# Quarter-array values, shared low-rank visits and shifted pieces in a streamed encoder layer on one Trainium2 core

## The chip, the cores and the metric

The kernel runs on one core of a Trainium2 chip. The metric is device time in microseconds (us); the number for a kernel is the median of its timed runs. One more execution is taken by the hardware profiler, and all times inside the kernel come from that one.

## What is computed

One encoder layer of width 2048 for 256 tokens. RMS-normed input `h` goes through one wide projection; three token mixers work on slices of it (windowed attention, a bidirectional RWKV-7 scan, cross-attention to 256 memory tokens); each result is gated, projected, weighted by a merge gate and summed; an output projection and a residual add close the layer. All in float32. The loop over both directions is the RWKV branch; the two products in it are the low-rank ones, and for each direction a scan over the tokens follows it, with a 64x64 state per head.

```python
h = rms_norm(x, norm_g)
proj = h @ w_in
...
mkv = rms_norm(mem, mem_norm_g) @ x_w_kv
...
for d in range(N_DIR):
    wd = -softplus(-(w0[d] + tanh(w_in[d]) @ w2[d])) - 0.5
    ad = sigmoid(a0[d] + a_in[d] @ a2[d])
    kd = k * (1.0 + (ad - 1.0) * k_a)
...
merged = gates[0] * (y_a @ attn_w_o) + gates[1] * (y_r @ rwkv_w_o) + gates[2] * (y_x @ x_w_o)
return x + merged @ w_out
```

## The kernel before

Nearly all of the work is products of 256 tokens with 160 MB of weights. The weights are cut into 277 **pieces**, each 128 partitions by 1024 numbers (512 KB); the first two are half as large (`planned(w_kv[0], KT, 512, 2)`: two single pieces of one k-tile). A piece passes through four stations:

- SyncE (SP) issues its DMA into one of four `raw` buffers (L172);
- ScalarE (ACT) rounds it to `w_hi` (L187), VectorE (DVE) computes the rest, `w_lo` (L191); four buffers of each;
- TensorE (PE) multiplies. In `stream_tok` tokens lie on the partitions of the result: per piece eight matmuls of 512 columns with `w_hi` (L287 and L288, with the high and low part of the activations) and four with `w_lo` (L280). The low products of a piece are issued one piece later (`late`), those of a stream's last piece at its end. `stream_feat` (L261, L262, L254) is the same with features on the partitions and 256 columns. Each stream has two accumulators, `ps[0]` and `ps[1]`, which `evac` takes away at its end.

After each piece `advance()` (L224) gives every background generator its turn: attention and, later, three RWKV batches b = 0, 1, 2 of four heads, one after the other. A generator that yields n sleeps for n pieces. What its steps put on PE stands between two pieces; I call it a **visit**. The order of PE and SP is the order of the code; on DVE and ACT too, after the attention part. There it matters that a step of a generator and the casts of the stream stand in one queue.

The steps of an RWKV batch that the change or the prediction names:

- norms of kk (L765), the low-rank products of the two head pairs (`low_rank(0)`, `low_rank(1)`, L777, evacuated by ACT tanh, L781), and the transposes of the norm (L795), with which DVE multiplies kk (L796);
- `prepare(d)` for each direction, in three blocks a piece apart. Block A: DVE sum and scan (L809, L812). Block B: ACT exponentials and kd (L817 to L821), then DVE kd (L823). Block C: DVE aa (L825) and four operations into BK (L829 to L832). `prepare(0)` of batch b+1 runs while batch b is in its state chain;
- `values()` (L854): 16 small products with the identity, which turn v to token order; ACT copies them into SV (L857, L858);
- products L877 and L880; the inversion of 64x64 blocks, first on DVE (L943, L946), then with X going out to memory (`td`) and back (L959), a transpose on DVE (L965, TP) and small products L971 and L978;
- the state chain over four chunks c of 64 tokens: Z (L1013, copied by DVE at L1015), U (L1023, copied into SV by DVE at L1025 and ACT at L1026), S (L1031, to Sn on DVE at L1035 and L1037, copied into SV by ACT at L1038 and DVE at L1039), each step a visit with a `yield 1` behind it. Each step needs the copy of the step before;
- outputs (L1004, L1007), norm and gate.

`ps_b` is the PSUM pool of these steps and has four buffers. `beside` (L161) holds the loads of memory and token rows (`araw`), each tied to the number of a piece: they are issued ahead of that piece. `WARM` matmuls on zeros (L328) stand ahead of everything on PE.

Of the kernel before, what the change touches and what calls it, by code (L numbers as in the profile page):

```python
# [8 lines left out]
F32 = mybir.dt.float32  # L9
# [8 lines left out]
P = 128  # L18
T = 256
DM = 2048  # L20
KT = DM // P
C = 64
NCH = T // C
# [26 lines left out]
RAWS = 4  # L50
HB = 4
LB = 4
WARM = 16

INV_STEP = 3

# [2 lines left out]
def tile_hybrid_layer(ctx: ExitStack, tc: tile.TileContext, x_tok, xT, memT, w_kv, wt, wq2, wf, wg, gate_b,  # L59
                      wo_a, wo_r, wo_x, w_out, lora, par, rowp, consts, out):  # L60
    nc = tc.nc
    V, S, G, TE = nc.vector, nc.scalar, nc.gpsimd, nc.tensor
# [25 lines left out]
    ident = cst[:, 0:128]  # L88
# [25 lines left out]
    def planned(w, kt, c, small=0, ks=None):  # L114

        n, ks = 1024 // c, ks or list(range(kt))
        for j in list(range(0, small)) + list(range(small, len(ks), n)):
            m = 1 if j < small else n
            plan.append((w[:, ks[j] : ks[j] + m, :], ks[j : j + m], c))
# [9 lines left out]
        planned(wo_x[c], 4, 512)  # L129


    planned(w_kv[0], KT, 512, 2)
    planned(w_kv[1], KT, 512)
    planned(wt[0], KT, 512)
    planned(wt[1], KT, 512)
# [135 lines left out]
    def stream_tok(kt, c, act, evac, ks=None):  # L271

        ah, al = act
        ps = [ps_acc.tile([P, 512], F32, name="acc") for _ in range(2)]
        ks = ks or list(range(kt))

        def low(lo, kl):
            for i in range(2):
                for k, kk in enumerate(kl):
                    TE.matmul(ps[i][:, 0:c], ah[:, kk, i * P : (i + 1) * P], lo[:, k, :], start=False, stop=(kk == ks[-1]))  # L280

        late = None
        for kl, hi, lo in pieces(c, ks):
            for i in range(2):
                for k, kk in enumerate(kl):
                    m = slice(i * P, (i + 1) * P)
                    TE.matmul(ps[i][:, 0:c], ah[:, kk, m], hi[:, k, :], start=(kk == ks[0]), stop=False)  # L287
                    TE.matmul(ps[i][:, 0:c], al[:, kk, m], hi[:, k, :], start=False, stop=False)  # L288
            if late is not None:
                low(*late)  # L290
            late = lo, kl
            advance()
        low(*late)
        for i in range(2):
            evac(i, ps[i][:, 0:c])


# [66 lines left out]
    ss4 = [apool.tile([P, 4, T], F32, name="ss4", bufs=1) for _ in range(2)]  # L364
    part_m = prep(memT, "mem_g", mT_, ss4[0], True)
    part_x = prep(xT, "norm_g", hT, ss4[1], False)
    for piece, k0, n in ((0, 0, 1), (1, 1, 1), (2, 2, 2), (3, 4, 4), (5, 8, 4), (7, 12, 4)):
        beside[piece] = [lambda k0=k0, n=n: part_m(k0, n)]
    for piece, k0 in ((11, 0), (13, 4), (16, 8), (18, 12)):
        beside[piece] = [lambda k0=k0: part_x(k0, 4)]  # L370

    kmT = apool.tile([P, 4, T], F32, name="kmT")
# [371 lines left out]
    def rwkv_batch(b):  # L744
# [4 lines left out]
        rp, kp, vp = (rkv[n, b] for n in "rkv")  # L749
# [22 lines left out]
        def low_rank(p):  # L772
            lps = [ps_b.tile([P, 512], F32, name="ps_b") for _ in range(2)]
            for j, s in enumerate((th, afT)):
                for d in range(2):
                    dr = slice(64 * d, 64 * d + 64)
                    TE.matmul(lps[d][:, j * T : (j + 1) * T], lw[dr, p, j, :], s[dr, :], start=True, stop=True)  # L777
            for d in range(2):
                f = rev if d else (lambda a: a)
                o = d * 6 + pps[p]  # L780
                S.activation(f(sgs[d][:, p, :]), lps[d][:, 0:T], AF.Tanh, bias=der[:, 52 + o : 53 + o], scale=0.5)  # L781
                S.activation(f(aas[d][:, p, :]), lps[d][:, T : 2 * T], AF.Tanh, bias=der[:, 64 + o : 65 + o], scale=0.5)

        yield 1
        low_rank(0)
        yield 2
        low_rank(1)
        rb = tpool.tile([P, 8, 64], F32, name="t1")
        S.copy(rb, rn.unsqueeze(2).broadcast_to([P, 8, 64]))
        yield 2  # L790
        rps = ps_b.tile([P, 2, T], F32, name="ps_b")
        for p in range(2):
            for t in range(2):
                o = 4 * p + 2 * t
                TE.transpose(rps[:, p, t * P : (t + 1) * P], rb[:, o : o + 2, :].rearrange("p a b -> p (a b)"), ident)  # L795
        V.tensor_tensor(kk, kk, rps, ALU.mult)  # L796
        yield 1

        def chs(ap):
# [46 lines left out]

        def values():

            vps = ps_b.tile([P, 2, NCH, 64], F32, name="ps_b")
            for p in range(2):  # L850
                for c in range(NCH):
                    for e in range(2):
                        er, orr = slice(64 * e, 64 * e + 64), slice(64 - 64 * e, 128 - 64 * e)
                        TE.matmul(vps[orr, p, c, :], vp[er, p, c * C : (c + 1) * C], ident[er, er], start=True, stop=True)  # L854
            for e in range(2):
                orr = slice(64 - 64 * e, 128 - 64 * e)
                S.copy(SV[e][orr, :, 0], vps[orr])  # L857
                S.copy(SV[e][orr, :, 1, ::-1], vps[orr])  # L858

        def arrive(d):  # L860
            f, E, BK = prep[d]
# [100 lines left out]
        yield 2  # L962

        TP = rpool.tile([P, 16, 32], F32, name="TP")
        V.transpose(TP.rearrange("p u s -> p (u s)"), Xu[:, :, 0:32])  # L965
        yield 1
        lo_, up = [slice(e * 64, e * 64 + 32) for e in range(2)], [slice(e * 64 + 32, e * 64 + 64) for e in range(2)]
# [41 lines left out]
        for c in range(NCH):  # L1009
# [6 lines left out]
            if c == NCH - 1:  # L1016
                yps += [ps_b.tile([P, 2, 2, 64], F32, name="ps_b") for _ in range(2)]
                outputs((1, 2))
            yield 1

            ups = [ps_b.tile([P, 2, 64], F32, name="ps_b") for _ in range(2)]
            for q, e in turns:
# [150 lines left out]
    for c in (3, 0, 1, 2):  # L1173
# [18 lines left out]
        def evac(i, ps, c=c, grt=grt, act=act):  # L1192
            gated(grt[:, i, :], ps)
            V.tensor_tensor(act[:, i, :], act[:, i, :], grt[:, i, :], ALU.add)
            start(merge(c, i, act))
# [100 lines left out]
```

## Time and profile before

| | us |
|---|---|
| timed runs (3) | 910.26, 910.92, 912.34 |
| median | 910.92 |
| profiled execution | 907.79 |
| its span | 906.0 |
| PE busy in the span | 893.4 |
| DVE busy | 648.2 |
| ACT busy | 456.9 |

In a row of the timeline stand the start, the busy time, engine, line, operation, output and inputs with their shapes, the number of instructions, and in brackets the idle time ahead of it with what ended that. The matmuls of PE overlap, so a matmul's time is read from one start to the next. L numbers are lines of the kernel before.

### The profile page before, as it was taken

What the parts mean: (1) busy time and instruction counts of PE and PEld (TensorE: products, weight loads), DVE (VectorE), ACT (ScalarE), POOL (GpSimd) and SP (SyncE); (2) the same over time, 40 slices, a digit from 0 to 9 for tenths busy, and PEclk for the clock granted to TensorE, in tenths of its full rate; (3) what the DMA queues carried; (4) which work ended last, traced back from release to release, by engine and by line L of the source; (5) the groups of instructions that cost most, each with busy time, mean ns of one, the idle gap of its engine ahead of it and who ended that gap; (6) DMA issues with size and microseconds to landing.
All of it is one profiled execution on the core that took longest, in us unless ns stands there. A gap on an engine that the chain in (4) does not pass through costs nothing.

```text
span 906.0 us, 15781 instructions
## 1 busy us (share of the span) xinstructions
PE 893.4 (99%) x6204; PEld 757.8 (84%) x6204; DVE 648.2 (72%) x1074; ACT 456.9 (50%) x690; POOL 89.5 (10%) x104
## 2 busy tenths in 40 slices
PE   8999999999999999999999999999999999999998
PEld 6788978999789999877899987788887778888886
DVE  6867687765488898666797955789796658586442
ACT  7766566655565544543554345355433435444331
POOL 2254231210100011100001110010000000000000
PEclk9999999999999999999999999999999999999999
DMA  8857644434656556644456575456768545787771
GB/s 303 268 195 252 199 140 137 141 120 136 185 179 206 165 177 191 183 128 145 146 180 216 162 235 147 129 165 185 223 198 244 163 152 176 238 272 233 233 234 66
DMA packets 67977, 168.66 MB, mean 186 GB/s; under 512 B 24448, under 2 KB 25984, under 8 KB 67904
## 3 DMA queue, kind: packets, MB, share of 16 engines
q1 hardware_dynamic: 42336, 150.75, 53.0%
q10 hardware_dynamic: 25568, 16.91, 6.5%
q8 instruction: 49, 0.80, 0.4%
q14 instruction: 24, 0.20, 0.1%
HBM read 160.82 MB, written 6.82 MB: 185 GB/s over the span
## 4 chain that ended last, share of the span: by engine, by line
PE 92%; DVE 3%; DMA 2%; issue 1%; ACT 1%; SPq 0%; ACTq 0%; DVEq 0%
PE acc L287 20%; PE acc L280 19%; PE acc L288 19%; PE acc L261 8%; PE acc L254 8%; PE acc L262 8%; PE ps_b L877 1%; DVE w_lo L191 1%; PE ps_t L448 1%; PE ps_b L880 1%; PE ps_b L1004 1%; DMA araw<-in_memT 1%; PE ps_s L544 1%; PE ps_b L777 1%; PE ps_b L1013 1%
## 5 line engine op out<-in xcount | busy, mean ns | idle before, releaser
L191 DVE TENSOR_TENSOR w_lo<-raw,w_hi 128x1024 fp32r<-128x1024 f32 (+1 forms) x277 | 342.2, 1248 | 94.9 <-PE acc L280 40.9
L187 ACT CAST w_hi<-raw 128x1024 fp32r<-128x1024 f32 (+1 forms) x277 | 286.5, 1046 | 200.3 <-PE acc L288 70.0
L287 PE MATMUL acc<-w_hi,hT 128*128 128x512 f32 (+1 forms) x512 | 200.1, 393 | 0.0
L288 PE MATMUL acc<-w_hi,hT 128*128 128x512 f32 (+1 forms) x512 | 195.3, 384 | 0.0
L261 PE MATMUL acc<-hT,w_hi 128*128 128x256 f32 x576 | 141.9, 285 | 0.2 <-DVE gx L1092 0.2
L262 PE MATMUL acc<-hT,w_hi 128*128 128x256 f32 x576 | 140.6, 283 | 0.0
L280 PE MATMUL acc<-w_lo,hT 128*128 128x512 f32 (+1 forms) x512 | 133.2, 385 | 0.0
L287 PEld LDWEIGHTS acc<-w_hi,hT 128*128 128x128 f32 x512 | 96.3, 188 | 21.0 <-issue 1.3
L261 PEld LDWEIGHTS acc<-hT,w_hi 128*128 128x128 f32 x576 | 110.3, 192 | 1.8 <-issue 1.7
L288 PEld LDWEIGHTS acc<-w_hi,hT 128*128 128x128 f32 x512 | 96.4, 188 | 17.5
L262 PEld LDWEIGHTS acc<-hT,w_hi 128*128 128x128 f32 x576 | 110.4, 192 | 0.1
L280 PEld LDWEIGHTS acc<-w_lo,hT 128*128 128x128 f32 x512 | 93.6, 188 | 19.0 <-issue 0.3
L254 PE MATMUL acc<-hT,w_lo 128*128 128x256 f32 x576 | 80.1, 285 | 0.0
L287 PE MATMUL acc<-w_hi,mT 128*128 128x512 f32 x192 | 76.7, 400 | 2.5 <-ACT w_hi L187 2.4
L288 PE MATMUL acc<-w_hi,mT 128*128 128x512 f32 x192 | 75.7, 394 | 0.0
L254 PEld LDWEIGHTS acc<-hT,w_lo 128*128 128x128 f32 x576 | 73.7, 192 | 0.9 <-issue 0.7
L280 PE MATMUL acc<-w_lo,mT 128*128 128x512 f32 x192 | 51.8, 395 | 0.0
L287 PEld LDWEIGHTS acc<-w_hi,mT 128*128 128x128 f32 x192 | 36.1, 188 | 13.0 <-ACT w_hi L187 4.3
L280 PEld LDWEIGHTS acc<-w_lo,mT 128*128 128x128 f32 x192 | 36.1, 188 | 8.7
L288 PEld LDWEIGHTS acc<-w_hi,mT 128*128 128x128 f32 x192 | 36.1, 188 | 8.2
L287 PE MATMUL acc<-w_hi,ya 128*128 128x512 f32 x96 | 38.1, 397 | 0.0
L288 PE MATMUL acc<-w_hi,ya 128*128 128x512 f32 x96 | 37.5, 390 | 0.0
(241 smaller groups left out, 981.1 us busy)
## 6 DMA issues: line engine op xcount, KB each, us to landing
raw<-in_wg SPq DMA_DIRECT2D x96, 512.0 KB, 3.8
raw<-in_wf SPq DMA_DIRECT2D x72, 512.0 KB, 4.0
raw<-in_w_out SPq DMA_DIRECT2D x32, 512.0 KB, 4.3
raw<-in_wt SPq DMA_DIRECT2D x24, 512.0 KB, 4.5
raw<-in_w_kv SPq DMA_DIRECT2D x15, 512.0 KB, 5.2
raw<-in_wo_a SPq DMA_DIRECT2D x12, 512.0 KB, 5.6
raw<-in_wo_r SPq DMA_DIRECT2D x12, 512.0 KB, 4.6
raw<-in_wo_x SPq DMA_DIRECT2D x8, 512.0 KB, 3.7
```

Source lines behind the costliest of these rows:

```text
L187: S.copy(hi_t[m], raw_t[m])
L191: V.tensor_tensor(lo_t[m], raw_t[m], hi_t[m].bitcast(F32), ALU.subtract)
L254: TE.matmul(ps[i][:, 0:T], lo[:, k, i * P : (i + 1) * P], ah[:, kk, :], start=False, stop=(kk == kt - 1))
L261: TE.matmul(ps[i][:, 0:T], hi[:, k, m], ah[:, kk, :], start=(kk == 0), stop=False)
L262: TE.matmul(ps[i][:, 0:T], hi[:, k, m], al[:, kk, :], start=False, stop=False)
L280: TE.matmul(ps[i][:, 0:c], ah[:, kk, i * P : (i + 1) * P], lo[:, k, :], start=False, stop=(kk == ks[-1]))
L287: TE.matmul(ps[i][:, 0:c], ah[:, kk, m], hi[:, k, :], start=(kk == ks[0]), stop=False)
L288: TE.matmul(ps[i][:, 0:c], al[:, kk, m], hi[:, k, :], start=False, stop=False)
L448: TE.transpose(ps[:, kt * T + t * P : kt * T + (t + 1) * P], pr[:, t, kt * P : (kt + 1) * P], ident)
L544: TE.matmul(s_ps[:, t, :], qT[r, pair, t * P : (t + 1) * P], kTt[r, g, :], start=True, stop=True)
L777: TE.matmul(lps[d][:, j * T : (j + 1) * T], lw[dr, p, j, :], s[dr, :], start=True, stop=True)
L877: TE.matmul(apss[e][:, c, :], BK[er, p, c, :], AR[er, p, d, c, :], start=True, stop=True)
```

## The change

Seven edits:

1. `WARM` goes from 16 to 22.
2. The first weight starts with four single pieces instead of two (278 pieces in all), and the keys of `beside` move up by one, so that each load stands ahead of the same weights.
3. `stream_tok`: at a stream's last piece the low products of the piece before are held back. The visit comes first, then for each accumulator the low products of both last pieces, then its evacuation.
4. `low_rank(0)` joins the visit of the norms, the transposes (L795) follow two pieces later, and `low_rank(1)` joins their visit. From the norms to block A three pieces pass (1, 1, 1) where six did (1, 2, 2, 1).
5. `values()` writes two PSUM tiles instead of one, in the order c, p, e, and the quarter of the array changes with each product: four in a row use four different quarters, where before two alternated. ACT copies eight halves instead of four wholes.
6. For b = 2 one more piece passes before the DVE transpose TP.
7. Behind Z of chunk 0 the generator sleeps two pieces instead of one, for b = 0 and 1.

```diff
-WARM = 16
+WARM = 22
...
-    planned(w_kv[0], KT, 512, 2)
+    planned(w_kv[0], KT, 512, 4)
...
-        def low(lo, kl):
-            for i in range(2):
-                for k, kk in enumerate(kl):
-                    TE.matmul(ps[i][:, 0:c], ah[:, kk, i * P : (i + 1) * P], lo[:, k, :], start=False, stop=(kk == ks[-1]))
-
-        late = None
+        def low(i, lo, kl):
+            for k, kk in enumerate(kl):
+                TE.matmul(ps[i][:, 0:c], ah[:, kk, i * P : (i + 1) * P], lo[:, k, :], start=False, stop=(kk == ks[-1]))
+
+        late = []
...
-            if late is not None:
-                low(*late)
-            late = lo, kl
+            if late and kl[-1] != ks[-1]:
+                l = late.pop(0)
+                for i in range(2):
+                    low(i, *l)
+            late.append((lo, kl))
             advance()
-        low(*late)
+
         for i in range(2):
+            for l in late:
+                low(i, *l)
             evac(i, ps[i][:, 0:c])
...
-    for piece, k0, n in ((0, 0, 1), (1, 1, 1), (2, 2, 2), (3, 4, 4), (5, 8, 4), (7, 12, 4)):
+    for piece, k0, n in ((0, 0, 1), (1, 1, 1), (2, 2, 2), (4, 4, 4), (6, 8, 4), (8, 12, 4)):
...
-        yield 1
         low_rank(0)
-        yield 2
-        low_rank(1)
+        yield 1
         rb = tpool.tile([P, 8, 64], F32, name="t1")
         S.copy(rb, rn.unsqueeze(2).broadcast_to([P, 8, 64]))
-        yield 2
+        yield 1
...
         V.tensor_tensor(kk, kk, rps, ALU.mult)
+        low_rank(1)
         yield 1
...
-            vps = ps_b.tile([P, 2, NCH, 64], F32, name="ps_b")
-            for p in range(2):
-                for c in range(NCH):
+            vps = [ps_b.tile([P, NCH, 64], F32, name="ps_b") for _ in range(2)]
+            for c in range(NCH):
+                for p in range(2):
                     for e in range(2):
-                        er, orr = slice(64 * e, 64 * e + 64), slice(64 - 64 * e, 128 - 64 * e)
-                        TE.matmul(vps[orr, p, c, :], vp[er, p, c * C : (c + 1) * C], ident[er, er], start=True, stop=True)
+                        er, o = slice(64 * e, 64 * e + 64), 64 * (1 - e ^ p)
+                        TE.matmul(vps[p][o : o + 64, c, :], vp[er, p, c * C : (c + 1) * C], ident[er, er], start=True, stop=True)
...
+        if b == 2:
+            yield 1
         V.transpose(TP.rearrange("p u s -> p (u s)"), Xu[:, :, 0:32])
...
-            yield 1
+            yield 2 if c == 0 and b < 2 else 1
```

What stands in the queues at three places. First VectorE at the hand-over from batch 0 to batch 1, chunk 1 to 2 of batch 0, before:

```order
L823 TENSOR_TENSOR kd<-kd,rs_k 128x512
L191 TENSOR_TENSOR w_lo<-raw,w_hi 128x1024
L1035 TENSOR_TENSOR Sn<-ps_b,Sn 128x256
L1037 TENSOR_TENSOR Sn<-Sn,EC 128x256
L1039 COPY SV_2825<-Sn 64x4x64
L825 SCALAR_TENSOR_TENSOR aa<-aa,kk 128x512
L829 SCALAR_TENSOR_TENSOR BK<-aa,Ei 64x8x64
L830 SCALAR_TENSOR_TENSOR BK<-aa,Ei 64x8x64
L831 TENSOR_TENSOR BK<-kd,Ei 64x8x64
L832 TENSOR_TENSOR BK<-kd,Ei 64x8x64
L191 TENSOR_TENSOR w_lo<-raw,w_hi 128x1024
L1015 COPY Z<-ps_b 128x256
```

and in the changed kernel, whose lines are numbered up to seven higher (SV copies L1032, Sn L1042 and L1044, Z L1022):

```order
L1032 TENSOR_SCALAR SV_2780<-ps_b 64x2x64 x2
L827 SCALAR_TENSOR_TENSOR aa<-aa,kk 128x512
L831 SCALAR_TENSOR_TENSOR BK<-aa,Ei 64x8x64
L832 SCALAR_TENSOR_TENSOR BK<-aa,Ei 64x8x64
L833 TENSOR_TENSOR BK<-kd,Ei 64x8x64
L834 TENSOR_TENSOR BK<-kd,Ei 64x8x64
L191 TENSOR_TENSOR w_lo<-raw,w_hi 128x1024
L1042 TENSOR_TENSOR Sn<-ps_b,Sn 128x256
L1044 TENSOR_TENSOR Sn<-Sn,EC 128x256
L1046 COPY SV_2781<-Sn 64x4x64
L191 TENSOR_TENSOR w_lo<-raw,w_hi 128x1024
L1022 COPY Z<-ps_b 128x256
```

Block C of batch 1 stood between the Sn of chunk 1 and the Z copy of chunk 2; it now stands between the SV copies and the Sn of chunk 1.

Second, VectorE at the hand-over from batch 1 to batch 2, before:

```order
L1039 COPY SV_4860<-Sn 64x4x64
L825 SCALAR_TENSOR_TENSOR aa<-aa,kk 128x512
L829 SCALAR_TENSOR_TENSOR BK<-aa,Ei 64x8x64
L830 SCALAR_TENSOR_TENSOR BK<-aa,Ei 64x8x64
L831 TENSOR_TENSOR BK<-kd,Ei 64x8x64
L832 TENSOR_TENSOR BK<-kd,Ei 64x8x64
L191 TENSOR_TENSOR w_lo<-raw,w_hi 128x1024
L1015 COPY Z<-ps_b 128x256
```

and now, from the last operations on the state of chunk 0 to the SV copies of chunk 1:

```order
L825 TENSOR_TENSOR kd<-kd,rs_k 128x512
L108 SCALAR_TENSOR_TENSOR ga<-ga,acc 128x512 x2
L191 TENSOR_TENSOR w_lo<-raw,w_hi 128x1024
L1022 COPY Z<-ps_b 128x256
L827 SCALAR_TENSOR_TENSOR aa<-aa,kk 128x512
L831 SCALAR_TENSOR_TENSOR BK<-aa,Ei 64x8x64
L832 SCALAR_TENSOR_TENSOR BK<-aa,Ei 64x8x64
L833 TENSOR_TENSOR BK<-kd,Ei 64x8x64
L834 TENSOR_TENSOR BK<-kd,Ei 64x8x64
L191 TENSOR_TENSOR w_lo<-raw,w_hi 128x1024
L1032 TENSOR_SCALAR SV_4831<-ps_b 64x2x64 x2
```

Here block C has moved from behind the state of chunk 1 to behind the Z copy of chunk 1, ahead of the SV copies of the same chunk; L108 is the stream's gating of an accumulator.

Third, TensorE at the first `values()`, before, with the numbers of the buffers:

```order
L280 MATMUL acc_2728<-w_lo_2732,hT0_94 128x512 x2
L280 MATMUL acc_2729<-w_lo_2732,hT0_94 128x512 x2
L854 MATMUL ps_b_2826<-cst_89,rs_v_2329 64x64 x16
L287 MATMUL acc_2728<-w_hi_2751,hT0_94 128x512
L288 MATMUL acc_2728<-w_hi_2751,hT1_95 128x512
```

and now:

```order
L287 MATMUL acc_2759<-w_hi_2678,hT1_95 128x512
L857 MATMUL ps_b_2782<-cst_89,rs_v_2341 64x64 x2
L857 MATMUL ps_b_2783<-cst_89,rs_v_2341 64x64 x2
L857 MATMUL ps_b_2782<-cst_89,rs_v_2341 64x64 x2
L857 MATMUL ps_b_2783<-cst_89,rs_v_2341 64x64 x2
L857 MATMUL ps_b_2782<-cst_89,rs_v_2341 64x64 x2
L857 MATMUL ps_b_2783<-cst_89,rs_v_2341 64x64 x2
L857 MATMUL ps_b_2782<-cst_89,rs_v_2341 64x64 x2
L857 MATMUL ps_b_2783<-cst_89,rs_v_2341 64x64 x2
L286 MATMUL acc_2758<-w_hi_2702,hT0_94 128x512
```

The 16 products went to one tile in one run; they now go to two tiles, two products each in turn. The first `values()` also stands behind the first piece of a stream now, where there is no earlier piece whose low products would stand ahead of it.

More of the change, by code (lines that the diff above doesn't have):

```diff
@@ L366, in tile_hybrid_layer @@
     part_x = prep(xT, "norm_g", hT, ss4[1], False)
-    for piece, k0, n in ((0, 0, 1), (1, 1, 1), (2, 2, 2), (3, 4, 4), (5, 8, 4), (7, 12, 4)):
+    for piece, k0, n in ((0, 0, 1), (1, 1, 1), (2, 2, 2), (4, 4, 4), (6, 8, 4), (8, 12, 4)):
         beside[piece] = [lambda k0=k0, n=n: part_m(k0, n)]
-    for piece, k0 in ((11, 0), (13, 4), (16, 8), (18, 12)):
+    for piece, k0 in ((12, 0), (14, 4), (17, 8), (19, 12)):
         beside[piece] = [lambda k0=k0: part_x(k0, 4)]
@@ L782, in low_rank @@
                 S.activation(f(aas[d][:, p, :]), lps[d][:, T : 2 * T], AF.Tanh, bias=der[:, 64 + o : 65 + o], scale=0.5)
+        low_rank(0)
         yield 1
-        low_rank(0)
-        yield 2
-        low_rank(1)
         rb = tpool.tile([P, 8, 64], F32, name="t1")
         S.copy(rb, rn.unsqueeze(2).broadcast_to([P, 8, 64]))
-        yield 2
+        yield 1
         rps = ps_b.tile([P, 2, T], F32, name="ps_b")
@@ L847, in values @@
         def values():
-            vps = ps_b.tile([P, 2, NCH, 64], F32, name="ps_b")
-            for p in range(2):
-                for c in range(NCH):
+            vps = [ps_b.tile([P, NCH, 64], F32, name="ps_b") for _ in range(2)]
+            for c in range(NCH):
+                for p in range(2):
                     for e in range(2):
-                        er, orr = slice(64 * e, 64 * e + 64), slice(64 - 64 * e, 128 - 64 * e)
-                        TE.matmul(vps[orr, p, c, :], vp[er, p, c * C : (c + 1) * C], ident[er, er], start=True, stop=True)
+                        er, o = slice(64 * e, 64 * e + 64), 64 * (1 - e ^ p)
+                        TE.matmul(vps[p][o : o + 64, c, :], vp[er, p, c * C : (c + 1) * C], ident[er, er], start=True, stop=True)
             for e in range(2):
                 orr = slice(64 - 64 * e, 128 - 64 * e)
-                S.copy(SV[e][orr, :, 0], vps[orr])
-                S.copy(SV[e][orr, :, 1, ::-1], vps[orr])
+                for p in range(2):
+                    o = 64 * (1 - e ^ p)
+                    S.copy(SV[e][orr, p, 0], vps[p][o : o + 64])
+                    S.copy(SV[e][orr, p, 1, ::-1], vps[p][o : o + 64])
         def arrive(d):
```

## The prediction

> **What bounds the kernel now.** I read the profile's own page first, for the engine that carries the span.
>
> ```profile
> span 906.0 us, 15781 instructions
> PE 893.4 (99%) x6204; PEld 757.8 (84%) x6204; DVE 648.2 (72%) x1074; ACT 456.9 (50%) x690; POOL 89.5 (10%) x104
> PEclk9999999999999999999999999999999999999999
> PE 92%; DVE 3%; DMA 2%; issue 1%; ACT 1%; SPq 0%; ACTq 0%; DVEq 0%
> ```
>
> TensorE is busy for 99% of the span, at a granted clock of 90% or more in all 40 slices, and holds 92% of the chain that ended last. The change takes no stream matmul away. So it can act in three ways only: through the waits of PE, through the time of the small matmuls between pieces (I call one such stop a visit), and through the two ends of the program. The second view is the table of PE's waits.
>
> ```profile
> PE ps_b L1023 <- DVE Z L1015: 2.7, 2, 1.3
> PE acc L287 <- ACT w_hi L187: 2.4, 3, 1.4
> ...
> PE ps_b L971 <- DVE TP L965: 0.7, 1, 0.7
> PE acc L261 <- DVE gx L1092: 0.2, 1, 0.2
> ```
>
> The columns are total, times, longest. All of it is some 7 us, of which the change touches every row shown here; nothing it does can be worth much more than that. The third view is PE's timeline around visits.
>
> ```profile
> 395.46 1.07 PE L280 MATMUL acc<-w_lo,hT 128*128 128x512 f32 x4
> 396.46 0.46 PE L1023 MATMUL ps_b<-Z,X 64*64 64x64 f32 x16
> 396.85 0.50 PE L287 MATMUL acc<-w_hi,hT 128*128 128x512 f32 x1
> 397.19 0.39 PE L288 MATMUL acc<-w_hi,hT 128*128 128x512 f32 x1
> ...
> 258.99 1.15 PE L854 MATMUL ps_b<-cst,rs_v 64*64 64x64 f32 x32
> 260.07 0.50 PE L287 MATMUL acc<-w_hi,hT 128*128 128x512 f32 x1
> ...
> 231.20 0.49 PE L287 MATMUL acc<-w_hi,hT 128*128 128x512 f32 x1
> 231.52 0.40 PE L288 MATMUL acc<-w_hi,hT 128*128 128x512 f32 x1
> ```
>
> I count from start to start, since the ends overlap. A stream matmul takes 0.23 (four in 0.93). After the four at 395.46 the visit should start at 396.39 and starts at 396.46: 0.07 to enter a smaller form. The first stream matmul behind it takes 0.34 instead of 0.23: 0.11. A trip into a small form and back thus costs about 0.18 besides its matmuls. The rows at 231.20 stand behind a visit of 128*128 form (L765): 0.32 instead of 0.23, so such a visit costs 0.09.
>
> **The change part by part.** All terms are against the profiled execution.
>
> *Values in fours.* L854 has 32 records and lasts 1.08 (258.99 to 260.07), L1023 has 16 and lasts 0.39. L1023 already names four different quarters in turn, L854 only two. If L854 runs two at a time and L1023 four, they are 16 and 4 sets: (1.08 - 0.39)/12 = 0.058 a set, with 0.16 to leave. If both ran in twos, they would be 16 and 8 sets of 0.086, and leaving would cost less than nothing (0.39 - 0.69). So I take fours as real: 8 sets fewer, 0.46 a visit, three visits: **-1.4** (bounds -1.4 and 0). The extra evacuations (eight ACT copies of half the size in place of four) lie on ACT, which is busy 50% of the span, ahead of work due several us later: nothing. Here a rule speaks against the change: the Trainium skill's page TensorEngine Tiling (Array Packing), Restrictions and Gotchas, Gotcha 1, says that different row tiles cannot access the same PSUM bank at the same time, and the new order lets both row halves write one bank back to back. By it the term would be 0. The two rows above disagree with it, since L1023 writes its banks in just that way and fits only as fours.
>
> *Low-rank products in shared visits.* For b=0 the same trips stay and two visits go: -0.1. For b=1 and b=2 both L777 groups rode in trips made anyway (L971, L1013), and L795 in that of L1031. Now L796 and the second group stand alone, and in the first shared visit PE goes from the small form to 128*128 (L768) and back to a small one: two trips more, 0.36, less 0.09 for the L765 visit that goes: +0.27 each. Sum **+0.4** (bounds 0 and +0.6). For b=1 the visit of L796 also asks for a fifth tile of a pool of four while U's two tiles are being drained; that can cost nothing or the 0.6 of the drain (SV row below): **+0.15**.
>
> *The two hand-overs between batches.* These are the 2.7 us of L1023, one wait each for b=0 to 1 and b=1 to 2. The rows are DVE, ACT and PE of the first.
>
> ```profile
> 396.96 0.61 DVE L1025 TENSOR_SCALAR SV<-ps_b 64x128 f32<-64x128 f32 x2 [0.19 <-PE ps_b L1023]
> 401.92 0.43 DVE L1035 TENSOR_TENSOR Sn<-ps_b,Sn 128x256 f32<-128x256 f32 x1
> 403.17 0.69 DVE L825 SCALAR_TENSOR_TENSOR aa<-aa,kk 128x512 f32<-128x512 f32 x1
> 405.99 0.69 DVE L832 TENSOR_TENSOR BK<-kd,Ei 64x512 f32<-64x512 f32 x1
> 406.71 1.23 DVE L191 TENSOR_TENSOR w_lo<-raw,w_hi 128x1024 fp32r<-128x1024 f32 x1
> ```
>
> ```profile
> 402.84 0.41 ACT L1038 COPY SV<-Sn 64x256 f32<-64x256 f32 x1 [1.88 <-DVE Sn L1037]
> ```
>
> ```profile
> 399.80 0.69 PE L1031 MATMUL ps_b<-SV,BKT 128*64 128x64 f32 x16
> ...
> 403.36 0.69 PE L1013 MATMUL ps_b<-SV,W 128*64 128x64 f32 x16
> ...
> 408.32 0.46 PE L1023 MATMUL ps_b<-Z,X 64*64 64x64 f32 x16 [1.33 <-DVE Z L1015]
> ```
>
> The five operations of the next batch's block C (L825 to L832) hold DVE from 403.17 to 406.68, 3.51 us, and a w_lo of 1.2 stands behind them; the small copy for which PE waits comes only then. A period between visits is 3.3 to 3.6. In the changed order C stands elsewhere, so the wait is worked out anew.
>
> b=0 to 1: C now follows U1's SV copies, ahead of the Sn of the same chunk. Counted from the start of U1 (396.46): SV ends at 1.11, C at 4.62, w_lo at 5.82, the Sn pair and the ACT copy (401.92 to 403.25) at 7.15. PE wants that copy two periods after U1, 403.36 - 396.46 = 6.90. Wait 0.3 in place of 1.33: **-1.0** (bounds -1.33 and -0.5).
>
> b=1 to 2: C now stands between Z1's copy and U1's SV copies. In front of Z1's copy come the products kd and the gated pair.
>
> ```profile
> 552.65 1.29 DVE L108 SCALAR_TENSOR_TENSOR ga<-ga,acc 128x512 f32<-128x512 f32 x2
> ...
> 565.93 0.69 DVE L823 TENSOR_TENSOR kd<-kd,rs_k 128x512 f32<-128x512 f32 x1 [2.50 <-ACT kd L821]
> ```
>
> Since kd waits for a chain on ACT, Z1's copy should come some 3.3 after Z1's matmuls (the rest of kd 0.6, L108 1.29, a w_lo 1.2, the copy), just when U1 wants it. Then C and w_lo take 4.7, the SV copies 0.8, to 8.8; the next visit S1 wants them two periods after Z1, at 6.9 to 7.0. Wait 1.8 in place of 1.33: **+0.5**. If kd and L108 are done early, the copy comes 1.1 after Z1 and C is hidden (wait 0); if a w_lo more slips in, 2.6 or over: bounds -1.33 and +1.3.
>
> *The gx evacuation at 452.94.* The wait of L261 stands behind the second block C of b=1, which now comes two pieces earlier: **-0.2**, its row in the table of waits.
>
> *The extra piece before the transpose of b=2.*
>
> ```profile
> 694.34 2.30 ACTq L1108 DMA_DIRECT2D acc_d<-gx  x1
> ...
> 698.96 0.70 DVE L965 STREAM_TRANSPOSE TP<-X 128x512 f32<-128x512 f32 x1
> ...
> 699.81 1.20 PE L971 MATMUL ps_b<-TP,X 32*32 32x32 f32 x64 [0.69 <-DVE TP L965]
> ```
>
> PE waits 0.69 for the transpose, late because a DMA issue held ACT's casts and with them DVE. The batch reaches that place a piece earlier now and then pauses a piece; X<-td is loaded earlier and the transpose has a visit more: **-0.7** (bounds -0.7 and, if the wait only moves, +0.4).
>
> *The two ends.* The start, PE and ACT:
>
> ```profile
> 1.13 3.60 PE L328 MATMUL ps_t<-zero 128*128 128x256 bf16 x16 [1.13 <-POOL zero L323]
> 6.17 0.50 PE L287 MATMUL acc<-w_hi,mT 128*128 128x512 f32 x1 [1.45 <-ACT w_hi L187]
> ...
> 25.53 1.10 PE L280 MATMUL acc<-w_lo,mT 128*128 128x512 f32 x4
> 26.71 0.50 PE L287 MATMUL acc<-w_hi,mT 128*128 128x512 f32 x1
> ```
>
> ```profile
> 24.66 1.06 ACT L346 ACTIVATE araw<-araw 128x1024 f32<-128x1024 f32 x1 [2.43 <-DVE mT L341]
> 25.63 2.92 ACT L187 CAST w_hi<-raw 128x1024 fp32r<-128x1024 f32 x3
> ```
>
> Six more warm-up matmuls at 0.225 end at 6.1, before the first cast lets PE start at 6.17: free. Smaller third and fourth pieces can give PE its weights sooner, up to the 2.4 less 1.4 of the table of waits. But at 26.71 PE is 0.25 late again (25.53 + 0.93 = 26.46), behind a cast that stands behind a square that waited for mT: a chain of ACT and DVE that does not wait for PE. What PE gains before, it waits there: **0** (bounds -0.5 and +0.6, the latter if the smaller buffers delay a load).
>
> The tail:
>
> ```profile
> 901.52 1.35 DVE L1206 SCALAR_TENSOR_TENSOR xr<-acc,xr 128x512 f32<-128x512 f32 x3 [7.58 <-PE acc L280]
> ```
>
> With both low products of accumulator 0 first, its evacuation starts two matmuls (0.46) sooner, and the second then waits for the last matmul instead of DVE: **-0.1** (bounds -0.4 and 0). In other streams visits move 0.9 ahead at a stream's end; no wait of the table lies there: 0.
>
> Sum: -1.4 + 0.4 + 0.15 - 1.0 + 0.5 - 0.2 - 0.7 - 0.1 = **-2.35**. The profiled execution took 907.79 us, 1.79 outside its span; the sum makes it 905.4. The timed runs before lie 2.5 to 4.6 above it (910.26 to 912.34), with nothing in the trace to say why; I keep the difference and take it from the median: 910.92 - 2.35 = **908.6**. What a measurement here tells from no change is about 0.2%, 1.8 us.
>
> **The rivals.** *C exposed at both hand-overs (slower).* In both new places C stands directly ahead of a copy that PE needs within two periods. The chain of 4.7 is hidden only as long as DVE is on time when C starts; for each us that DVE is late there, PE waits one more. Without hand-overs the sum is -1.85; with waits of 3.5 at each it is -1.85 + 7.0 - 2.7 = +2.5, **913.4**. It decides from 3.2 us each. For it: L108 and kd ahead of C, and DVE's 72%. Against: in the first hand-over the count gives 0.3, far off. Chance 0.09.
>
> *The gains are eaten (same).* The wait of b=1 to 2 comes out at 2.6 and the transpose's wait only moves: -2.35 + 0.8 + 0.7 = -0.85, **910.1**. Chance 0.24.
>
> *C hidden in the second hand-over.* -2.35 - 1.8 = -4.15, **906.8**. For it: Z1's copy needs only 1.1 after its matmuls when DVE is free. Chance 0.13.
>
> *Values do not run in fours*, so that the reordering does nothing: -0.95, **910.0**. The only evidence against it is the fit of the two rows above. Chance 0.05. The Trainium skill's page TensorEngine Tiling (Array Packing), Gotcha 1, would have it come out so.
>
> *A start at a lower clock in other executions.* The profiled start has full spacing at 6.17 already, but 1.45 us of idle lie between warming and stream, and other executions are slower by 3. If the first ten stream matmuls (2.3 us) ran at half speed there, warming on to 6.1 would save 2.3, less the 0.25 of slack at 26.71 and what else the chain there takes up, say 1.8: **906.8**. The Trainium skill's page TensorE: Matmul & The Clock Gate, Part 1, has such a rule: a free-running window of about 3.4 us sets the clock, so that the warm-up differs between runs. This trace, at 0.9 or more from its first slice, shows none of it. Chance 0.07.
>
> **How the numbers follow.** The forecast's own case has 0.42. Faster by over 0.2% (under 909.1): most of the forecast's case 0.36, hidden C 0.13, the clock 0.07: 0.56. Within 0.2%: the rest of the forecast's 0.06, eaten gains 0.24, no fours 0.05: 0.35. Slower: 0.09. The range goes down to 905.9, under the two cases at 906.8, and up to 911.2, over those at 910.1 with 1.1 for unknown costs; it leaves out the slower case and the tails of the others.
>
> **What would show it right or wrong.** Right: the values visit lasts 0.6 instead of 1.08; L1023's waits of 1.3 are gone and waits of L1013's or L1031's successors (for SV copies) stand there, about 0.3 near 405 and 1.8 near 570; L971's and L261's rows vanish from the table of waits; PE waits near 26.5 as long as it gained before; the last evacuation begins 0.1 after the last matmul. Wrong: a values visit of 1.08, either hand-over over 2.6, a new wait of L978 or of the transposes in a shared visit, or a stream start at 26.7 that is earlier by more than 0.3.

## The result and the profile after

The changed kernel is slower. Its six timed runs lie between 912.40 and 917.05 us, median 915.22; the kernel before, on the same chip, has 911.63 (908.66 to 912.52). The ratio is 1.0062, 95% interval 1.0044 to 1.0080. The forecast was 908.6 with a range of 905.9 to 911.2: wrong in sign. The profiled execution took 912.40 us, against 907.79 before. The page:

```profile
span 910.3 us, 15810 instructions
PE 895.1 (98%) x6210; PEld 758.4 (83%) x6210; DVE 650.7 (71%) x1075; ACT 459.2 (50%) x703; POOL 91.3 (10%) x104
PEclk9999999999999999999999999999999999999999
PE 81%; DVE 6%; DMA 6%; issue 2%; ACT 2%; POOL 1%; ACTq 1%; SPq 0%; DVEq 0%
```

PE's work is about what it was (895.1 against 893.4; six more warm-up matmuls at 0.21 are 1.3 of it), the span is 4.3 longer, and PE's share of the last chain fell from 92% to 81%: the loss is waiting. The table of PE's waits (total, times, longest; lines numbered up to seven higher than before):

```profile
PE acc L286 <- ACT w_hi L187: 3.2, 5, 1.3
PE ps_b L978 <- DVE TP L972: 2.5, 2, 2.0
PE ps_s L547 <- ACT qT L462: 1.9, 2, 1.2
PE ps_b L1038 <- DVE SV L1032: 1.2, 1, 1.2
...
PE ps_t L451 <- DVE s_pr L444: 0.7, 1, 0.7
PE ps_b L1020 <- ACT SV L1045: 0.2, 1, 0.2
```

What was forecast is there: the 2.7 us of U behind Z are gone, 0.2 and 1.2 stand in their place (0.3 and 1.8 were forecast), and the rows of L971 at b=2 and of gx are gone. But three rows are new or longer that no step of the prediction had: the transpose TP is awaited 2.5 us, at b=0 and b=1 where it never was; the query copy takes 1.9 instead of 1.4, and the probabilities 0.7.

To see where the time goes I set the start of one and the same stream matmul against its start in the first profile. In us, at six places of the kernel before, for the changed kernel (two profiles; the second is run e11 below) and the unchanged kernel again (e4):

| place before | after | after again | before again |
|---|---|---|---|
| 55.3 | +2.71 | +0.66 | +0.67 |
| 108.4 | +2.51 | +0.32 | +0.67 |
| 143.0 | +4.22 | +2.00 | +0.67 |
| 483.5 | +2.69 | +0.43 | +0.65 |
| 645.9 | +4.95 | +2.58 | +0.67 |
| 895.3 | +4.20 | +1.83 | +0.60 |

Two things can be read from it. What the first profile lost in the first 55 us is not in the second, so it is not the change. And 1.7 us are lost between 108 and 143 (attention) and 2.2 between 483 and 646 (the inversion of b=1 and the second hand-over) in both; between 143 and 483 it gains 1.5, and behind 646 0.75.

From 108 us on, the waits account for it. PE's listed waits there sum to 4.9 us before, 6.6 and 6.4 in the two profiles after. The visits behind 150 us, each taken from the last stream matmul ahead of it to the first behind it, less that matmul's own time and less waits, take 98.1 us before (both profiles) and 98.2 after (both): they gained nothing.

The visit of the values and the two hand-overs, on PE:

```profile
254.85 0.69 PE L857 MATMUL ps_b<-cst,rs_v 64*64 64x64 f32 x32
255.47 0.50 PE L286 MATMUL acc<-w_hi,hT 128*128 128x512 f32 x1
...
402.83 0.69 PE L1020 MATMUL ps_b<-SV,W 128*64 128x64 f32 x16 [0.21 <-ACT SV L1045]
...
569.22 1.19 PE L1038 MATMUL ps_b<-SV,BKT 128*64 128x64 f32 x16 [1.19 <-DVE SV L1032]
```

The values last 0.62 where they lasted 1.08: 0.46 a visit, as forecast. That is the time of four quarters at once by the prediction's count, although both row halves write one bank. The Trainium skill's page TensorEngine Tiling (Array Packing), Restrictions and Gotchas, Gotcha 1, says that different row tiles cannot access the same bank at the same time; here that costs nothing, and the measurement decides.

Now the new wait, at b=1. First ScalarE before, then after; ACTq rows are the issue of DMAs from its queue, in which everything waits for what stands ahead.

```profile
521.89 1.25 ACTq L954 DMA_DIRECT2D td<-IN  x2
523.18 2.38 ACTq L753 DMA_DIRECT2D lw<-in_lora  x2
...
527.08 2.08 ACT L187 CAST w_hi<-raw 128x1024 fp32r<-128x1024 f32 x2
528.80 2.51 ACTq L959 DMA_DIRECT2D X<-td  x4
```

```profile
519.71 1.25 ACTq L959 DMA_DIRECT2D td<-IN  x2
...
526.86 1.93 ACTq L964 DMA_DIRECT2D X<-td  x4
528.83 2.52 ACTq L756 DMA_DIRECT2D lw<-in_lora  x2
531.39 0.91 ACT L761 ACTIVATE kk<-rs_k,prm 128x256 f32<-128x256 f32 x2 [4.73 <-issue]
532.33 0.63 ACT L762 ACTIVATE t<-kk 128x512 f32<-128x512 f32 x1
...
532.87 2.92 ACT L187 CAST w_hi<-raw 128x1024 fp32r<-128x1024 f32 x3
```

VectorE and PE before, then after:

```profile
534.45 0.71 DVE L965 STREAM_TRANSPOSE TP<-X 128x512 f32<-128x512 f32 x1 [0.71 <-DMA X<-td]
```

```profile
537.61 1.20 PE L971 MATMUL ps_b<-TP,X 32*32 32x32 f32 x64
```

```profile
533.94 1.23 DVE L191 TENSOR_TENSOR w_lo<-raw,w_hi 128x1024 fp32r<-128x1024 f32 x1 [6.02 <-DMA lw<-in_lora]
535.08 0.70 DVE L972 STREAM_TRANSPOSE TP<-X 128x512 f32<-128x512 f32 x1
```

```profile
535.93 1.20 PE L978 MATMUL ps_b<-TP,X 32*32 32x32 f32 x64 [1.96 <-DVE TP L972]
```

In the kernel before, the next batch's loads lw and its kk step filled the time in which td went out. X was asked for 8.8 us ahead of L971 (528.80 to 537.61); the transpose waited for X until 534.45, and TP was still done with 2.4 to spare. With the low-rank steps three pieces shorter the inversion ends earlier in the stream, before the inputs of the next batch are there (rs_v, L589, comes at 523.75, behind td's issue at 519.71). That batch starts only behind X's loads, and lw's issue, kk and the square stand ahead of the stream's casts: ScalarE casts nothing from 526.7 to 532.87, VectorE is idle for 6.0, and its w_lo holds TP. And X is asked for only 7.1 us before PE wants TP (526.86 to 533.97).

### The profile page after: what moved, and what is told of

Same layout as the page of the kernel before. It is cut to its first block, busy times and chain, and to the rows that moved or that the text cites. A ratio compares the mean times of both kernels' runs of the same rounds, so it can differ in the third digit from the quotient of the medians.

```text
span 910.3 us, 15810 instructions
## 1 busy us (share of the span) xinstructions
PE 895.1 (98%) x6210; PEld 758.4 (83%) x6210; DVE 650.7 (71%) x1075; ACT 459.2 (50%) x703; POOL 91.3 (10%) x104
## 4 chain that ended last, share of the span: by engine, by line
PE 81%; DVE 6%; DMA 6%; issue 2%; ACT 2%; POOL 1%; ACTq 1%; SPq 0%; DVEq 0%
PE acc L286 18%; PE acc L279 17%; PE acc L287 17%; PE acc L261 6%; PE acc L262 6%; PE acc L254 6%; DVE w_lo L191 3%; PE ps_b L882 1%; DMA araw<-in_xT 1%; DMA raw<-in_w_kv 1%; ACT w_hi L187 1%; DMA raw<-in_wf 1%; PE ps_t L451 1%; PE ps_b L885 1%; PE ps_b L1011 1%
## 5 line engine op out<-in xcount | busy, mean ns | idle before, releaser
L279 PE MATMUL acc<-w_lo,hT 128*128 128x512 f32 (+1 forms) x512 | 131.2, 384 | 0.0
```

## The experiments

The experiments ran on three other chips. Every ratio is against the kernel before on the same chip, whose medians there are 909.28 (e1 to e4), 908.78 (e5 to e8) and 908.57 us (e9 to e11).

**e1: edits 1 and 2 alone.**

```diff
-WARM = 16
+WARM = 22
...
-    planned(w_kv[0], KT, 512, 2)
+    planned(w_kv[0], KT, 512, 4)
...
```

> The kernel before with edits 1 and 2 alone (22 warm-up matmuls; four single pieces, load keys moved by one). Theory: the smaller pieces fill the same four raw buffers with half the bytes, so later weights and the loads of memory and token rows start and land later; the chain load, cast, w_lo, square to the last token rows reaches PE 2.7 us later at piece 17 (58.0 against 55.3 us), and nothing gives it back: +2.5 to +2.9 us at the end, a stall of about 1.4 us at 56 us. Rival: the late loads of the changed kernel's profile were chance of that execution; then the same place is reached within 0.5 us of before, and the end too.

Measured: ratio 1.0008 (0.9994 to 1.0022); +0.37 at 55 us, +1.22 at the end, of which 0.6 is a longer wait of L971 at b=2 (1.3 where 0.7 stood), far from the edits. The theory falls. **e4: the kernel before again.**

> The kernel before, unchanged, as a control for what differs between two profiled executions. Both theories: every piece starts within 0.5 us of the first profile at full clock, and the time is within 0.2% of before. If loads at the start land over 1 us apart, differences of that size at the start of single profiles mean nothing.

Measured: 1.0009 (0.9992 to 1.0026), and its profile is +0.67 at 55 us: more than the 0.5 expected, and more than e1. This is the noise against which all else stands: about 0.1% in a ratio (with an interval up to 0.26%), and 0.7 us or more at the start of one profile (e9 below, with the start's pieces as before, had +2.5). Edits 1 and 2 make no difference that can be seen.

**e2: edit 3 alone** (stream_tok as in the diff above, nothing else).

```diff
-            if late is not None:
-                low(*late)
-            late = lo, kl
+            if late and kl[-1] != ks[-1]:
...
```

> The kernel before with edit 3 alone (low products of a stream's last two pieces held back, the visit ahead of them). Theory: visits at stream ends come 0.93 us earlier, and the queues of VectorE and ScalarE in the attention part come out in another order; PE then waits 1.1 us for the probabilities near 127 us and 0.5 us more for the query copy near 139 us: +1.5 us by 143 us, kept to the end but for what the later visits change (within 0.7 us). Rival: the order of those queues does not matter, and the waits there come from the late start alone; then no shift over 0.3 us by 143 us.

Measured: 1.0007 (0.9997 to 1.0018). Its profile loses 1.67 us between 108 and 143 (+0.21 to +1.88) and has +1.62 at the end; so do all runs with edit 3, at that place (1.67 to 1.71 in five profiles), and none without it (0.03 at most). The mechanism is as stated. Its timed cost alone lies within the noise. VectorE at the place, first in the kernel before, then in the changed kernel's first profile, and there PE:

```profile
125.87 1.21 DVE L191 TENSOR_TENSOR w_lo<-raw,w_hi 128x1024 fp32r<-128x1024 f32 x1
127.00 0.15 DVE L439 RECIPROCAL s_rd<-s_den 128x2 f32<-128x2 f32 x1
127.08 0.13 DVE L437 TENSOR_TENSOR s_den<-s_den,s_es 128x2 f32<-128x2 f32 x1
127.19 0.61 DVE L441 TENSOR_SCALAR s_pr<-s_pr,s_rd 128x256 f32<-128x256 f32 x2
```

```profile
129.57 0.16 DVE L442 RECIPROCAL s_rd<-s_den 128x2 f32<-128x2 f32 x1
129.64 1.21 DVE L191 TENSOR_TENSOR w_lo<-raw,w_hi 128x1024 fp32r<-128x1024 f32 x1
130.76 0.15 DVE L440 TENSOR_TENSOR s_den<-s_den,s_es 128x2 f32<-128x2 f32 x1
130.83 0.61 DVE L444 TENSOR_SCALAR s_pr<-s_pr,s_rd 128x256 f32<-128x256 f32 x2
```

```profile
131.33 1.44 PE L451 MATMUL ps_t<-cst,s_pr 128*128 128x128 f32 x8 [0.72 <-DVE s_pr L444]
```

The w_lo stood ahead of the reciprocals; it now stands between the first of them and the scaling of the probabilities, for which PE waits. Here the order of VectorE is not the code's but a scheduler's, and edit 3 gave it other times to plan with.

**e3: edits 4 to 7 alone.**

```diff
-        yield 1
         low_rank(0)
-        yield 2
-        low_rank(1)
+        yield 1
...
-            yield 1
+            yield 2 if c == 0 and b < 2 else 1
```

> The kernel before with edits 4 to 7 alone (low-rank visits, values in fours, the pieces at Z and before the transpose). Theory: the values visits fall by 0.45 us each, the first hand-over wait falls to 0.3 us, the wait of L971 at b=2 goes, but the transpose TP of b=1 is awaited for about 2 us (b=0: 0.5 us), since ScalarE's queue holds the loads of lw and X ahead of the casts: in all -0.5 to +0.5 us. Rival: those waits come from the visits at stream ends being 0.9 us earlier (edit 3), so without it they are under 1.0 us in sum, and the kernel is 1.5 to 2.5 us faster than before.

Measured: 1.0041 (1.0024 to 1.0057), slower by about 3.7 us; TP is awaited 3.8 us in two waits, with no edit 3 in it, so the rival falls. The theory had the wait in the right place, 2.5 us of it where 3.8 came, and the price too low. PE behind the second wait, and the windows around it (us, PE busy, granted clock, DMA share, GB/s):

```profile
534.82 1.20 PE L975 MATMUL ps_b<-TP,X 32*32 32x32 f32 x64 [2.28 <-DVE TP L969]
535.95 0.74 PE L287 MATMUL acc<-w_hi,hT 128*128 128x512 f32 x1
536.49 0.63 PE L288 MATMUL acc<-w_hi,hT 128*128 128x512 f32 x1
...
539.47 1.07 PE L280 MATMUL acc<-w_lo,hT 128*128 128x512 f32 x4
```

```profile
532.00:536.00 4.00, 1.72 (x68) 1.00 0.46 130
536.00:540.00 4.00, 4.00 (x12) 0.57 0.80 247
540.00:544.00 4.00, 4.00 (x85) 1.00 0.28 102
```

Behind the wait the clock is down: the profile's record of the granted clock has 0.50 from 536.04 to 539.45, eight stream matmuls take 0.43 instead of 0.23, and 1.6 us are lost on top of the 2.3 of the wait. I call this a **spell**. Both TP waits of e3 (1.6 and 2.3) were followed by one, both of e7 (2.6 and 1.3), that of e5 (2.1), and a wait of 2.3 at 56 us in e9. The 2.0 and 1.8 of the changed kernel's own two profiles were not, nor one of 1.8 at 57 us in e7, nor the two of 1.33 in the kernel before. Between the first 12 us and the end of PE's work no spell stood without a wait of 1.3 or more ahead of it.

What decides can be read from the record. Every spell lasts 3.41 us, and within each trace all changes of the granted clock stand a whole number of 3.413 us apart: from the first spell to the second 170.67 us, 50 times that, in e3 and in e7 alike. So the windows run on by themselves, and the idle time counts that falls into one of them. In each row stand the idle time of PE in one window (3.41 less its busy time) and whether a spell filled the next:

| run, window (us) | PE idle | spell behind it |
|---|---|---|
| e7, 366.43 to 369.84 | 2.4 | yes |
| e9, 54.25 to 57.66 | 2.2 | yes |
| e3, 532.63 to 536.04 | 2.2 | yes |
| e5, 363.51 to 366.92 | 1.8 | yes |
| e7, 55.82 to 59.23 | 1.8 | no |
| e11, 529.93 to 533.34 | 1.6 | no |
| e3, 361.96 to 365.38 | 1.6 | yes |
| e7, 537.10 to 540.51 | 1.3 | yes |
| after, 534.81 to 538.22 | 1.1 | no |

The 2.0 of the changed kernel was cut by a window's edge into 0.84 and 1.12; that it had no spell is luck. In the two rows with a spell behind 1.6 and 1.3 the 1.1 us of 32x32 matmuls (L975, L979) behind the wait lie in the same window; it may be that they count for less than stream matmuls, which is not shown (they lie in the last row's window too). Windows of other runs with 1.2 to 1.4 us of idle, which the table leaves out, had no spell.

The timed runs of the changed kernel fit this: the profiled one, at clock 1.000, took 912.40, the others, at clocks of 0.998 down to 0.993, 914.69 to 917.05. One spell of 3.41 us at half the clock lowers the mean over 912 us by 0.0019, so these would be one to four spells, an estimate. The Trainium skill's page TensorE: Matmul & The Clock Gate, Part 1, has a free-running window of about 3.4 us and a clock that is halved after an idle one. The traces agree in the length, the halving and the free running; but 1.3 to 2.4 us of idle in a window were enough here, and the measurement decides.

**e5: edit 4 alone.**

```diff
-        yield 1
         low_rank(0)
-        yield 2
-        low_rank(1)
+        yield 1
...
         V.tensor_tensor(kk, kk, rps, ALU.mult)
+        low_rank(1)
```

> The kernel before with edit 4 alone (low-rank products in shared visits). Theory: it moves each batch's inversion three pieces ahead of the stream, so that the next batch's inputs are not there yet when the inversion ends; lw's loads and the kk step fall behind X's loads in ScalarE's queue and hold the casts, and less time stays from the load of X to the transpose. PE waits for TP about 1.5 us at b=0, 2.5 at b=1 and 1 or more at b=2, each wait of about 2 us followed by some 3.4 us in which stream matmuls take 0.43 instead of 0.23 us (1.5 us more): +4 to +8 us. Rival: the waits of e3 come from the moved pieces at Z and from the values, not from edit 4; then TP is awaited under 1 us in all, and the time is within 1 us of before.

Measured: 1.0042 (1.0028 to 1.0056). One listed wait for TP of 2.1 us, at b=0, with a spell behind it; the hand-over waits of 2.7 stay, and two more for the copies of S (1.3) come. TP is not awaited at b=1 and b=2, where 2.5 and 1 or more were expected. The visits take 99.0 us against 98.1 before, 0.9 more on PE alone. So edit 4 alone makes the kernel slower by the amount of e3, with the wait at one batch of the three expected. Two of its four timed runs stand at a clock of 1.000 and took 912.05 and 912.39, so most of the loss is there without a spell.

**e6: the pause before TP for every batch.**

```diff
         TP = rpool.tile([P, 16, 32], F32, name="TP")
-        if b == 2:
-            yield 1
+        yield 1
         V.transpose(TP.rearrange("p u s -> p (u s)"), Xu[:, :, 0:32])
```

> The changed kernel with the extra piece before TP for every batch, not for b=2 alone. Theory (the waits for TP are what the change loses by): no wait for TP over 0.3 us at b=0 and b=1, no clock loss behind them, 2.5 us less in a profile than the changed kernel and 3 to 5 us less in timed runs, so within 0.2% of before. Rival (the loss is at the start and in the attention part): at most 1 us less than the changed kernel, 0.4% or more above before.

Measured: 1.0017 (1.0003 to 1.0031) where the changed kernel has 1.0062; the profile's span is 906.6 (910.3 and 907.9). Its waits:

```profile
PE ps_s L547 <- ACT qT L462: 1.9, 2, 1.2
...
PE ps_b L1019 <- ACT SV L1044: 0.9, 1, 0.9
PE ps_t L451 <- DVE s_pr L444: 0.7, 1, 0.7
PE ps_b L1037 <- DVE SV L1031: 0.7, 1, 0.7
PE acc L261 <- DVE gx L1098: 0.4, 1, 0.4
```

In its profile no wait for TP is left, and no spell. One line gives back 0.45 of the 0.62%, though the hand-overs, which move with it, now cost 1.6 together and the wait for gx is back. The intervals of the two ratios do not overlap, and the rival, 0.4% or more above before, falls: the waits for TP are the main cause, shown.

**e7: lw's loads ahead of the wait for the inputs.**

```diff
         if b:
             yield from after(("inverted", b - 1))
+        pps = (2 * b, 2 * b + 1)
+        lw = tpool.tile([P, 2, 2, P], F32, name="lw")
+        for p in range(2):
+            nc.scalar.dma_start(out=lw[:, p], in_=lora[pps[p]])
         yield from after(("inputs", b))
...
```

> The changed kernel with lw's loads issued as soon as the inversion of the batch before is out, ahead of the wait for the inputs, so that they stand ahead of X's loads in ScalarE's queue as they do in the kernel before. Theory, first form (ScalarE's queue is held by lw's issue): the wait for TP at b=1 falls from 2.0 to under 1.1 us (X lands then), 1 to 3 us less than the changed kernel. Rival form (X's own landing sets TP): the wait at b=1 stays within 0.4 us of 2.0.

Measured: 1.0035 (1.0017 to 1.0052). The wait at b=1 fell to 1.3, that at b=0 rose to 2.6. Neither form holds. VectorE at b=0:

```profile
367.99 0.71 DVE L973 STREAM_TRANSPOSE TP<-X 128x512 f32<-128x512 f32 x1 [2.63 <-DMA X<-td]
```

Here the transpose waits for X itself. X's loads, 64 KB each, land in a median of 5.1 us after their issue at this place and of 7.4 us at b=1 (5.8 and 5.1 in the changed kernel's first profile). The transpose reads the columns of X that the first and third of the four loads fill. At b=1 of the changed kernel's first profile the third landed at 533.81 by the trace, and the transpose began at 535.08: of the wait of 2.0 about 1.3 is the held queue, and the rest is that td's way out and back no longer fits into the pieces it has. In e3 at b=1 the third load landed at 531.35 and the transpose began at 533.97, so there the queue was the whole wait; at b=0 of the changed kernel it landed at 365.60 and the transpose began at 365.62, so there X was. How long a load takes differs from run to run, and with it which of the two comes last.

**e10: e6 without edit 3.** The stream order of before, edits 1, 2 and 4 to 7, and the pause for every batch.

> The kernel of e6 (changed kernel, pause before TP for all) without edit 3, so with the stream order and the attention queues of before. Theory: the 1.4 us that PE loses between 108 and 143 us in every run with edit 3 go; the time is 1.0 to 1.5 us below e6 and within 0.1% of before. Rival: what is lost there is regained at later stream ends, so that the two are alike.

Measured: 1.0001 (0.9985 to 1.0017), against 1.0017 for e6: some 1.4 us less, as expected, but on another chip and with intervals that overlap, so the timed gain is not shown. Between 108 and 143 its profile loses 0.02, e6's 1.67: that part is. A wait of 0.5 for TP stands at b=2.

**e11: the changed kernel again**, unchanged, for its second profile (the table above).

> The changed kernel, unchanged, for a second profile. Theory: the waits for TP at b=0 and b=1 and the 1.5 us of the attention part come again (within 0.8 us each). What the first 60 us lose (2.7 us in the first profile, 0.4 in e1 and 1.0 in e6, 3.0 in e7) differs from run to run; if it comes near 2.7 again, edits 1 and 2 cost it together with edit 3. The clock falls behind one or both waits, or not at all.

Measured: 910.12 us in its one run, at a clock of 1.000 and 1.6 above that chip's median before; TP awaited 2.3 us (longest 1.8), the attention part +1.68, the first 55 us +0.66. The first part of the theory holds; the start does not repeat.

**e8: what the forecast had right, without edit 4.** Edits 1, 5 and 6, and the prelude of b=1 and b=2 a piece earlier, which puts block C between U's and S's copies at both hand-overs.

```diff
...
-        yield 4 if b else 2
+        yield 3 if b else 2
...
```

> The kernel before with edit 1 (warm-up), edit 5 (values in fours), edit 6 (a piece before TP for b=2), and the wait ahead of the norms of b=1 and b=2 one piece shorter, so that block C stands between U's and S's copies at both hand-overs, as it does in the changed kernel at the first. Theory: values -1.4, both hand-over waits 0.3 instead of 1.4 (-2.2), TP of b=2 -0.7, one low-rank group alone in a visit +0.4: -3.9 us, 0.4% faster than before. Rival (the time is set by start and clock, not by these waits): within 0.15% of before.

Measured: 0.9977 (0.9968 to 0.9987), 2.1 us faster. Half of the expected gain: the hand-over waits are 0.4 us together, TP is not awaited, but a new wait stands behind the last batch's norm, which comes a piece later with the pause for b=2:

```profile
762.12 0.63 PE L1073 MATMUL ps_b<-cst,ysum 128*128 128x128 f32 x4 [1.23 <-DVE ysum L1066]
```

**e9: e8 with one more piece there.**

```diff
-        yield 1 if b == 2 else 2
+        yield 2
```

> The kernel of e8 with one piece more ahead of the transposes of the last batch's norm, for which PE waited 1.6 us near 760 us there. Theory: that wait goes and nothing takes its place; profile 1.5 us below e8 when both starts are alike, 0.35 to 0.45% faster than before. Rival (the wait moves to the gates or to the last streams, which need that batch's result): no gain over e8, 0.2 to 0.25% faster than before.

Measured: 0.9960 (0.9947 to 0.9974), median 905.48 against 908.57: 3.1 to 3.6 us faster than before and the fastest of all. The wait is gone and none came in its place; the table of waits, without the rows of the start:

```profile
PE ps_s L544 <- ACT qT L459: 1.4, 2, 0.7
...
PE ps_b L1018 <- ACT SV L1043: 0.4, 2, 0.2
PE acc L261 <- DVE gx L1097: 0.2, 1, 0.2
```

Its span of 905.9 is no lower than before's because that one execution lost 3.8 us in its first 108 us, mostly in a wait of 2.3 for a cast at 56 us with a spell behind it.

## Why the prediction was wrong

*Values (-1.4): right*, 0.46 a visit. The argument named against it, two row halves in one bank, could not tell the two orders apart: in the order before, too, they write one tile in turn (`orr` changes with `e`). *First hand-over (-1.0): right*, wait 0.2 (forecast 0.3). *Second hand-over (+0.5): right in kind*, 1.2 (forecast 1.8, bounds 0 and 2.6). *gx (-0.2) and the transpose of b=2 (-0.7): right*, both rows gone, 0.75 gained behind 646 us. *Start (0): right* within what two profiles of one kernel differ there; the changed kernel's first profile would have misled me, the second and e1 did not. *Tail (-0.1)*: too small to tell. *The fifth tile (+0.15)*: no such wait stands in the table.

*Low-rank products in shared visits (+0.4): this is the step that failed.* I counted its visits on PE and nothing else. The step takes three pieces out of each batch, and the prediction used that only for the hand-overs. What it moves against the stream is also the inversion's way through memory (td, X), the start of the next batch, whose condition is the stream's, and their places in ScalarE's queue. I had the row that should have warned me: the 0.69 of L971 at b=2 is this wait, in the one batch with no spare time before; the change gives b=2 a pause, and I did not ask why the others should do without. It cost 2.5 us of waits, and through the clock some 1.6 more for each spell in the runs where one followed. e5 (edit 4 alone, 1.0042) and e6 (pause for all, 1.0017) show it. The count on PE was too low as well: the values save 1.4 and all visits together nothing (98.1 and 98.2), so the shared visits and the moved pieces take 1.4 back where +0.4 stood; edit 4 alone (e5) takes 0.9, over the bound of 0.6.

*The bound ahead of the terms.* That nothing the change does can be worth much more than the 7 us of PE's waits holds for waits that go. It says nothing of waits that come, and the range had 1.1 us of room for them. A new wait of L978 stood among the signs of being wrong, without a price.

*Stream ends ("no wait of the table lies there: 0"): failed, +1.7 us in the profile.* One visit at a stream's end does hold a wait, that of the query copy (1.4 in the table of before, a row that I left out), and 0.93 us less ahead of it made it 1.9. The larger part, 1.1, came from the scheduler's new order of VectorE in the attention part, which could be read off the order of the queues and which I looked at only around the RWKV batches.

*The slower rival* (block C exposed at both hand-overs, 913.4) named nearly the time that came, by a mechanism that did not come: the hand-overs cost 1.4 together. *The rival of a lower clock* had the right mechanism at the wrong place: the clock falls behind waits in mid-kernel, and a spell adds some 1.6 us to a wait of 1.3 to 2.6. A wait of 2 us was priced at 2.

*Open:* what the small matmuls count for in a window, and how much of the timed 1.0062 is spells. An estimate of that: the mean clock of the six timed runs is 0.9963, that of the 71 timed runs of the kernel before on the three other chips 0.9990 (on the first chip none is listed). The difference is 1.4 spells at 0.0019, some 2.3 us of the 5.7. What edit 3 costs in timed runs lies between nothing and 0.2%.

## What to carry to other kernels

When a step in a chain of background work gets shorter, list every wait that comes behind it in the same chain, loads through memory and conditions set by other work included, and ask for each how much spare time it had; a wait that already shows in one repetition is the one that will show in all. Where a scheduler sets the order of an engine, compare that order over the whole program and not only beside the edit. And price a wait of TensorE of over about 1.3 us at its length plus the chance of some 1.6 us at half the clock behind it; one profile without a spell does not show that the other executions have none.

## What the runs showed of the hardware

The granted clock fell to 0.50 for 3.41 us (0.43 us for a matmul of 0.23) behind every wait of 2.1 us or more between the start and the end (2.1, 2.3, 2.3, 2.6), behind some shorter ones (1.3, 1.6) and not behind others (1.3, 1.4, 1.8, 1.8, 2.0). The changes stand on a grid of 3.413 us in every trace; behind the start, windows with 1.84 us of idle or more were all followed by a spell, windows with 1.75 or less only where small matmuls lay in them too. At the start stream matmuls were 0.43 apart until about 10.4 us in e2 and e3, with 16 warm-up matmuls; this came in none of the profiles with 22 and not in the other three with 16. It cost nothing that can be seen: by 27 us both stood at +0.12, less than the +0.33 of the unchanged kernel's second profile; the prediction's reason, that PE waits there for a cast that does not depend on it, fits this. 16 products of 64x64, with both row halves writing one bank, took 0.62 us in four quarters where they took 1.08 in two. Loads of 64 KB took a median of 4.7 to 7.4 us to land beside the weights.
